# Group 0's rows of an MoE layer gathered on chip by one-hot products, with the other routes under its first expert

## The chip, the cores and the metric

The kernel runs on one core of a Trainium2 chip. The metric is device time in microseconds (us), the median of several executions. TensorE (PE) multiplies matrices, its weight loads are listed as PEld; VectorE is DVE, ScalarE ACT, GpSimd POOL, and SyncE (SP) issues most DMAs.

## What is computed

One layer of a decoder trunk on 512 tokens of 1024 features, all in fp32. A mixer (three branches and an output projection) gives a residual x1; then comes a mixture of experts in two steps. The most likely of 4 groups is chosen for a token, then 2 of its 4 experts:

```python
x = x + gt1 * mix
h2 = rms_norm(x, g_norm2) * (1.0 + sc2) + sh2
grp_prob = softmax(h2 @ w_group + b_group);  p_g, g_idx = top_k(grp_prob, 1)
sel_logits = (h2 @ w_router + b_router) of the 4 experts of g_idx
top_vals, e_idx = top_k(sel_logits, 2);  weights = p_g * softmax(top_vals)
for e in 16 experts:      # feature sizes 1024 -> 256 -> 1024
    y += (silu(h2 @ w_gate[e]) * (h2 @ w_up[e]) * combine[:, e]) @ w_down[e]
x = x + gt2 * y
```

`sc2`, `sh2`, `gt2` come from the condition c: a gain and a shift of each feature. With the inputs used, group 0 has 68 tokens, and no expert has more than two tiles of 128.

## The kernel before, in words

**Products.** fp32 products are exact enough in two ways. Either an operand is split into a high and a low fp32r half (`split`: ACT writes the high half, DVE subtracts to get the low one) and TensorE makes three passes (`mm3`, L216), or the operands stay fp32 ("native", one product listed as two records).

**The end of the mixer.** `out_mm(t, g, ...)` makes the block of token tile t (0 to 3) and output columns g (0 to 3) of the output projection; the order of blocks is the list `seq`, which ends (2, 2), (2, 3), (3, 2), (3, 3). After a block, `out_evac` (L1215, L1216) multiplies it by the gate and adds it to x1 on DVE; `x1_t` transposes a tile of x1 on TensorE (L1224) and ACT copies it (L1227); `logits` multiplies it by the router's weights, into which the gain is folded (L1236); `norm2` gives 1/rms of a token, rs2, whose power is taken on POOL (L1249); `norm_lg` scales the logits (L1252). `tile_chain(t)` is this series for one tile, put between blocks by a queue of generators (`wv`), a step or two behind the blocks. `h2_rows` makes half a tile of h2 rows (512 columns) and writes it to `h2_d` in DRAM; by its mode the work is on DVE, ACT or POOL (`h2_gain`, L1256, and L1275 are POOL's).

**The routes.** `route(t0)` finds group and experts of tiles t0 and t0 + 1 on DVE with some 15 small steps (L1290 to L1308). `ranks` (L1609, L1610) counts on TensorE, by products with a triangle and ones, which place a token has in its expert. Then DVE makes positions (L1654 to L1657), `weights` (L1312 to L1321) and `lightest` (L1640 to L1650: which of groups 1 to 3 has the fewest tokens; its experts share a tile at the end). `busy(n)` puts n products of ones between these steps on TensorE (L1399), whose result nobody reads; there are 41.

**The experts.** There are 17 passes e = 0 to 16. Passes 0 to 3 are the experts of group 0, pass 6 takes what overflows a tile, and passes 13 to 16 are the lightest group's, sharing a tile (`GL` = 13). For an expert with a tile of its own, `one_hot(e)` compares places with 0 to 127 on DVE (L1469); `slot_rows`/`slots` multiply it by token numbers and weights (L1477, L1488), and POOL gathers the rows from `h2_d` by an indirect DMA (L1481). `x_rows` transposes them, 8 transposes with a step of 8 elements (L1519), into `XTf` (native) or `XTh`/`XTl` (split). `gate_up` (L1535 or L216), `activate` (SiLU on ACT, L1543 on DVE), `act_t` (transpose of the activations, L1551), `down` (L1577 or L216), the scaling y (L1582) and an indirect DMA that adds the rows to the output (L1591) follow. `w_units` split the next expert's weights (L225, L226: `guh`, `gul`, `dnh`, `dnl`), pieces of 512 KB that SP loads in a fixed order into a ring of buffers (`load_raw`, L1167). Each engine takes its instructions strictly in the order in which the program's text emits them (`manual_schedule`), so the loop over e, which calls these parts in turn, is the order on every engine.

Of the kernel before, what the change touches and what calls it, by code (L numbers as in the profile page):

```python
# [35 lines left out]
PRE = 4  # L36
# [135 lines left out]
def trunk(ctx: ExitStack, tc: tile.TileContext, I, out, dbg=None):  # L172
# [793 lines left out]
    def mod_rows(hf):  # L966
# [18 lines left out]
        for j in range(4):  # L985
# [14 lines left out]
            if hf == (j < 2):  # L1000
                A.dma_start(mod_d[1 - hf:2 - hf, 512 * (j % 2):512 * (j % 2) + 512], bm[0:1])
            yield 1

    def router_consts():
        lst = sml("lst")[:, 0:128]
        A.dma_start(lst, I["cst"][:, C_LST:C_END])
        A.dma_start(R.mcol, mod_d.rearrange("a (k p) -> p a k", p=128))
        yield 5
# [8 lines left out]
        V.scalar_tensor_tensor(R.mcol[:, 0], R.mcol[:, 0], 1.0, pv[:, PV_G2:PV_G2 + 8], OP.add, OP.mult)  # L1017
# [165 lines left out]
    def f():  # L1183
# [17 lines left out]
        R.xg = pool("xgp", wps).tile([128, 1024], FT, name="xg")  # L1201
# [31 lines left out]
    def logits(t, ks, last=7, b=None):  # L1233
        b = b or bank()
        for k in ks:
            T.matmul(b[:, 0:27], xT.pop((t, k)), R.wrs[:, k], start=k in (0, 4), stop=k in (3, 7))  # L1236
        if 3 in ks:
            V.tensor_copy(R.LG[:, t], b[:, 0:27])
        elif 7 in ks:
            V.tensor_tensor(R.LG[:, t], R.LG[:, t], b[:, 0:27], OP.add)  # L1240
        return b
# [9 lines left out]
    def norm_lg(t):  # L1251
        V.scalar_tensor_tensor(R.LG[:, t], R.LG[:, t], R.rs2[:, t:t + 1], R.brb, OP.mult, OP.add)  # L1252

    def h2_gain(t, c0, n):
        c = slice(c0, c0 + n)
        G.tensor_tensor(R.xg[:, c], X1(t)[:, c], st["mod", 1][:, c], OP.mult)  # L1256

    def h2_rows(t, hf, mode):
        s = slice(hf * 512, hf * 512 + 512)
        s2 = slice(1024 + hf * 512, 1024 + hf * 512 + 512)  # L1260
        h2 = sml("h2")
        rs, sh = R.rs2[:, t:t + 1], st["mod", 0][:, s2]
        if mode[0] == "V":
            V.scalar_tensor_tensor(h2, X1(t)[:, s], rs, st["mod", 1][:, s], OP.mult, OP.mult)
        elif mode == "A":
            A.activation(h2, X1(t)[:, s], AF.Copy, scale=rs)
            G.tensor_tensor(h2, h2, st["mod", 1][:, s], OP.mult)
        elif mode == "gA":
            A.activation(h2, R.xg[:, s], AF.Copy, scale=rs)
        if mode == "gV":  # L1270
            V.scalar_tensor_tensor(h2, R.xg[:, s], rs, sh, OP.mult, OP.add)
        else:

            def end(eng=G):
                eng.tensor_tensor(h2, h2, sh, OP.add)  # L1275
                SY.dma_start(h2_d[t * 128:(t + 1) * 128, s], h2)
            if mode == "VV":
                return lambda: end(V)
            end()
            return  # L1280
        SY.dma_start(h2_d[t * 128:(t + 1) * 128, s], h2)
# [4 lines left out]
    def route(t0):  # L1286
# [3 lines left out]
        V.tensor_reduce(m1[:, :, 0:1], lg[:, :, 0:4], AX.X, OP.max)  # L1290
# [32 lines left out]
    def tile_chain(t):  # L1323
        x1_t(t, 512, 512)
        norm_pre(t)
        norm2(t)
        out_rows(t)
        yield 2 if t < 2 else 1
        logits(t, range(4, 8))
        norm_lg(t)  # L1330
        if t == 1:
            route(0)
        yield 1
        h2_rows(t, 1, "A" if t < 1 else "V")
        if t < 2:
            h2_rows(t, 0, "V")
        else:
            st["h2"] = h2_rows(t, 0, "VV")

    def last_half():  # L1340
        x1_t(3, 512, 256)
        h2_gain(3, 512, 256)
# [22 lines left out]
    def f():  # L1365
# [3 lines left out]
        for t, g in seq:  # L1369
# [27 lines left out]
    def busy(n):  # L1397
        for _ in range(n):
            T.matmul(wb, ones_c, ones_c[:, None, :].to_broadcast([128, 4, 128]), start=True, stop=True)  # L1399

    wb = bank("mm")
    lb = logits(3, (4, 5))
    busy(3)
# [59 lines left out]
    NE = 17  # L1463

    def one_hot(e, po=None):
        if po is None:
            po = R.PC[:, e, 0:4] if e < PRE else R.eb[:, 0:4] if e == EX else R.posx if e == EX + 1 else R.posL if e == GL else R.PP[:, wset(e) - PRE, 0:4]
# [5 lines left out]
    def slot_rows(e, b=None):  # L1473
# [21 lines left out]
    def slots(e):  # L1495
        if e < GL:
# [4 lines left out]
        for ti in range(NT):  # L1501
            T.matmul(b[:, 0:8], oh[:, ti], R.twL[:, ti], start=ti == 0, stop=ti == 3)
# [390 lines left out]
```

## Time and profile before

| | us |
|---|---|
| median of 3 runs | 809.42 (806.77 to 811.06) |
| the profiled execution | 806.46 |
| its span, first to last instruction | 804.6 |
| TensorE busy in the span | 759.2 (94%) |
| DVE busy | 558.0 (69%) |
| ACT busy | 313.5 (39%) |
| POOL busy | 177.8 (22%) |
| DMA, mean over the span | 185 GB/s |

The mean granted TensorE clock of the span is 0.985 of full speed. The page gives busy time per engine, a table of slices and groups of instructions; stretches and timelines are asked of the trace. Times in the rows count from the span's start. A record in brackets is the idle time before an instruction and what ended it.

### The profile page before, as it was taken

Reading aid. Unit: us, or ns where it says so; the run is one execution under the profiler, and the core shown is the slowest. Engines: PE = TensorE matmul, PEld = TensorE weight load, DVE = VectorE, ACT = ScalarE, POOL = GpSimd, SP = SyncE. Lnnn points to the kernel's source line nnn. Section 1 sums busy time; section 2 is a strip of 40 time slices with the busy share of each in tenths; the row PEclk is TensorE's granted clock in tenths of the full one; section 3 lists DMA queues with packets and bytes.
Section 4 is the critical chain, followed back from the end, with each engine's and each line's share of the span. In section 5 each row is a group of like instructions: output and inputs, shape, how many; then the busy total and the mean of one; then the engine's idle time right before and its main releaser. Section 6 shows DMA issues by size and latency. Waiting matters only on the chain. (4 is left out here: it accounts for less than half of the span.)

```text
span 804.6 us, 11741 instructions
## 1 busy us (share of the span) xinstructions
PE 759.2 (94%) x4261; PEld 628.2 (78%) x4262; DVE 558.0 (69%) x1046; ACT 313.5 (39%) x556; POOL 177.8 (22%) x162
## 2 busy tenths in 40 slices
PE   7699997999999999999899999999988999999994
PEld 4477986998888899998688887889975677777662
DVE  5987737778748776775777777745476788677761
ACT  5424743242334224322344333434212454355550
POOL 2522207422121013320110031300161223221100
PEclk9799999999999999999999999999989999999998
DMA  9882243221212121358445576597556999999931
GB/s 300 255 260 90 67 129 136 77 78 59 73 53 94 64 79 53 100 190 253 139 144 163 173 229 219 163 304 234 214 185 242 321 345 363 363 363 354 331 97 27
DMA packets 68596, 148.53 MB, mean 185 GB/s; under 512 B 8189, under 2 KB 35986, under 8 KB 68282
## 3 DMA queue, kind: packets, MB, share of 16 engines
q1 hardware_dynamic: 59234, 130.00, 47.4%
q0 software_dynamic: 4032, 14.68, 7.2%
q10 hardware_dynamic: 5272, 3.09, 1.4%
q8 instruction: 34, 0.56, 0.3%
q14 instruction: 24, 0.20, 0.1%
HBM read 136.21 MB, written 12.86 MB: 185 GB/s over the span
## 5 line engine op out<-in xcount | busy, mean ns | idle before, releaser
L226 DVE TENSOR_TENSOR wlo<-raw,whi 128x1024 fp32r<-128x1024 f32 x70 | 92.2, 1321 | 60.6 <-ACT whi L225 60.5
L216 PE MATMUL bank_mm<-whi,hTh 128*128 128x256 f32 x352 | 100.9, 287 | 0.0
L216 PE MATMUL bank_mm<-wlo,hTh 128*128 128x256 f32 x352 | 98.8, 281 | 1.8 <-DVE wlo L226 1.8
L216 PE MATMUL bank_mm<-whi,hTl 128*128 128x256 f32 x352 | 98.8, 281 | 0.0
L216 PE MATMUL bank_mm<-hTh,whi 128*128 128x512 f32 x224 | 92.4, 413 | 0.0
L225 ACT ACTIVATE whi<-raw 128x1024 fp32r<-128x1024 f32 x70 | 73.2, 1054 | 48.6 <-DMA raw<-in_w_t_dram 30.5
L216 PE MATMUL bank_mm<-hTh,wlo 128*128 128x512 f32 x224 | 88.9, 397 | 0.0
L216 PE MATMUL bank_mm<-hTl,whi 128*128 128x512 f32 x224 | 88.4, 395 | 0.0
L216 PEld LDWEIGHTS bank_mm<-wlo,hTh 128*128 128x128 f32 x352 | 66.4, 189 | 2.2 <-DVE wlo L226 2.0
L216 PEld LDWEIGHTS bank_mm<-whi,hTh 128*128 128x128 f32 x352 | 66.4, 189 | 0.6 <-issue 0.3
L216 PEld LDWEIGHTS bank_mm<-whi,hTl 128*128 128x128 f32 x352 | 66.3, 188 | 0.0
L216 PE MATMUL bank_mm<-whi,mgs 128*128 128x256 f32 x256 | 51.5, 295 | 0.2 <-DVE mgs L229 0.2
L216 PEld LDWEIGHTS bank_mm<-hTh,whi 128*128 128x128 f32 x224 | 42.2, 188 | 11.0 <-issue 1.0
L216 PEld LDWEIGHTS bank_mm<-hTh,wlo 128*128 128x128 f32 x224 | 42.1, 188 | 10.6 <-DVE wlo L226 0.5
L216 PEld LDWEIGHTS bank_mm<-hTl,whi 128*128 128x128 f32 x224 | 42.1, 188 | 10.0 <-issue 0.7
L216 PE MATMUL bank_ms<-dnh,aT 128*128 128x512 f32 x120 | 45.8, 441 | 0.0
L963 DVE SCALAR_TENSOR_TENSOR acc<-raw,c_act,acc 128x1024 f32<-128x1024 f32 x28 | 37.9, 1368 | 8.3 <-DMA raw<-in_w_mod_dram 7.9
L1591 POOL DMA_INDIRECT out_dram<-modb,idx x14 | 25.2, 1797 | 81.1 <-DVEq L1875 27.1
L216 PEld LDWEIGHTS bank_mm<-whi,mgs 128*128 128x128 f32 x256 | 42.6, 199 | 0.5 <-DVE mgs L229 0.4
L216 PE MATMUL bank_mm<-wlo,mgs 128*128 128x256 f32 x128 | 37.2, 291 | 0.0
L900 POOL TENSOR_TENSOR mg<-mg,ut 128x512 f32<-128x512 f32 x8 | 11.2, 1409 | 101.3 <-DVE ut L898 101.3
L1582 DVE SCALAR_TENSOR_TENSOR modb<-bank_ms,wsl,modb 128x512 f32<-128x512 f32 x26 | 19.5, 751 | 18.3 <-PE bank_ms L216 16.3
(439 smaller groups left out, 1798.0 us busy)
## 6 DMA issues: line engine op xcount, KB each, us to landing
raw<-in_w_t_dram SPq DMA_DIRECT2D x35, 512.0 KB, 3.5
raw<-in_w_mod_dram SPq DMA_DIRECT2D x32, 512.0 KB, 4.5
raw<-in_w_m_dram SPq DMA_DIRECT2D x24, 512.0 KB, 3.2
wmod<-in_w_mod_dram SPq DMA_DIRECT2D x16, 512.0 KB, 7.4
raw_x<-in_w_ed_dram SPq DMA_DIRECT2D x16, 512.0 KB, 9.2
raw_x<-in_w_eg_dram SPq DMA_DIRECT2D x15, 512.0 KB, 9.9
raw_x<-in_w_eu_dram SPq DMA_DIRECT2D x15, 512.0 KB, 8.5
raw_e<-in_w_eg_dram SPq DMA_DIRECT2D x14, 512.0 KB, 5.9
```

Of the source, the lines that this page charges most:

```text
L216: T.matmul(o, l[a], r[b], start=first and i == 0, stop=last and i == 2)
L225: A.activation(hi, src, AF.Copy)
L226: (eng or V).tensor_tensor(lo, src, hi.bitcast(FT), OP.subtract)
L900: G.tensor_tensor(m, m, u, OP.add)
L963: V.scalar_tensor_tensor(acc[:, c], raw, c_act[:, kt:kt + 1], acc[:, c], OP.mult, OP.add)
L1582: V.scalar_tensor_tensor(y[:, c], b, wsl_[e][:, 0:1], g, OP.mult, OP.mult)
L1591: G.indirect_dma_start(out, bass.IndirectOffsetOnAxis(idx_[e][:, 0:1], 0), y, None, compute_op=OP.add)
```

## The change

**Group 0 shares a tile.** Passes 0 to 3 work on one tile of group 0's tokens. `group(t)` marks on DVE which tokens of a tile have group 0, `group_ranks(t)` counts their places on TensorE, `group_hot(t)` makes on DVE a one-hot of token by place, already scaled by rs2. `gather(t)` multiplies x1 of the tile (stationary, columns k, k + 8, ...) by it, 8 products into two PSUM banks that add up over the four tiles; so the gathered rows come transposed, with no DMA and no transposes. `x_group` puts gain and shift on them with 8 ACT copies (`mcolx`, loaded by a DMA of its own), `x_halves` splits them for experts 1 to 3. The tile's 4 experts take its weights in `activate` (as the lightest group's do), their `down` products add up in the same two banks, and one scaling and one scatter follow after pass 3.

**The routes go under expert 0.** route(0) is called two blocks later, at (3, 2); route(2), the last ranks, positions, weights, lightest, the one-hot of pass 0 and the h2 rows of tiles 2 and 3 are emitted within pass 0, the steps of `overflow` in passes 0 and 1. Loads 16, 17, 20 and 21 are issued in the bridge, 18 and 19 after the h2 rows of tile 3.

**Row arithmetic.** `h2_rows` is on DVE alone, two steps for half a tile; `h2_gain` and `busy` are gone. POOL keeps the powers of rs2 and the indirect DMAs.

```diff
-    def h2_rows(t, hf, mode):
...
+    def h2_rows(t, hf):
         s = slice(hf * 512, hf * 512 + 512)
...
+        V.scalar_tensor_tensor(h2, X1(t)[:, s], R.rs2[:, t:t + 1], st["mod", 1][:, s], OP.mult, OP.mult)
+        V.tensor_tensor(h2, h2, st["mod", 0][:, 1024 + hf * 512:1536 + hf * 512], OP.add)
         SY.dma_start(h2_d[t * 128:(t + 1) * 128, s], h2)
+    def group(t):
+        m1 = R.MT[:, 0, t, 0:1]
+        V.tensor_reduce(m1, R.LG[:, t, 0:4], AX.X, OP.max)
+        V.tensor_tensor(R.gm[:, t], R.LG[:, t, 0:2], m1.to_broadcast([128, 2]), OP.is_equal)
+        V.tensor_scalar(R.pen[:, t:t + 1], R.gm[:, t, 0:1].bitcast(FT), -1024.0, 1024.0, OP.mult, OP.add)
+    def group_ranks(t):
...
+        for tj in range(t + 1):
+            T.matmul(st["rg"][:, 2 * t:2 * t + 2], R.lst if tj == t else ones_c, R.gm[:, tj], start=tj == 0, stop=tj == t)
+    def group_hot(t):
+        p0 = R.p0[:, t:t + 1]
+        V.tensor_tensor(p0, st["rg"][:, 2 * t:2 * t + 1], R.pen[:, t:t + 1], OP.add)
+        V.tensor_scalar(st["oh0"][:, t], R.cst[:, C_IOTA:C_IOTA + 128], p0, R.rs2[:, t:t + 1], OP.is_equal, OP.mult)
+    def gather(t, ks=range(8)):
...
+        for k in ks:
+            T.matmul(st["X0"][k // 4][:, (k % 4) * 128:(k % 4) * 128 + 128], X1(t)[:, k::8], st["oh0"][:, t],
+                     start=t == 0 and k % 4 == 0, stop=t == 3 and k % 4 == 3)
...
             if (t, g) == (3, 2):
                 wv.start(last_half(), 1)
+                route(0)
+                gather(0)
...
+    gather(1, range(5))
+    x1_t(3, 768, 256)
+    norm2(3)
+    gather(1, range(5, 8))
+    logits(3, (6, 7), b=lb)
+    norm_lg(3, lb)
+    group(3)
+    ranks((0, 1))
+    gather(2, range(3))
+    group_ranks(3)
+    group_hot(3)
+    gather(2, range(3, 8))
+    gather(3)
+    x_group()
+    out_rows(3)
+    for u in U:
+        u()
+    for j in (16, 17, 20, 21):
+        load_raw(j)
     route(2)
...
         gate_up(e, (0, 1))
         if e == 0:
+            x_halves()
         U[0]()
         U[1]()
+        if e == 0:
+            ranks((2, 3))
+            positions()
+            weights()
...
         gate_up(e, (2, 3))
         if e:
             act_t(e - 1)
+        if e == 0:
+            lightest()
...
+            one_hot(0)
...
         gate_up(e, (4, 5))
+        if e == 0:
+            slots(0)
+            h2_rows(2, 0)
+            h2_rows(2, 1)
...
         activate(e)
+        if e == 0:
+            h2_rows(3, 0)
+            h2_rows(3, 1)
+            for j in (18, 19):
+                load_raw(j)
...
+            one_hot(4)
```

Three places show what moved. First TensorE (PE) from the last ranks to the first gate_up products, before (L1477 are the index products, L1519 the transposes):

```order
L1399 MATMUL bank_mm<-ones_c 128x512 x8
L1477 MATMUL bank_ms<-tok,oh 128x4 x4
L1399 MATMUL bank_mm<-ones_c 128x512 x5
L1477 MATMUL bank_ms<-tok,oh 128x4 x4
L1399 MATMUL bank_mm<-ones_c 128x512 x12
L1519 MATMUL bank_ms<-ident,X 128x128 x8
L1477 MATMUL bank_ms<-tok,oh 128x4 x4
L1535 MATMUL bank_mm<-raw_e,XTf 128x512 x4
```

and from the last 13 gather products (L1282) through pass 0 with the change (L1613 and L1614 are `ranks((2, 3))`, L1547 `gate_up`, L1474 and L1499 `slots(0)`):

```order
L1282 MATMUL bank_ms<-oh_5545,x_5001 128x128 x13
L1547 MATMUL bank_mm<-raw_e,XTf 128x512 x2
L1613 MATMUL bank_mm<-mem,lst 128x20
L1613 MATMUL bank_mm<-mem,ones_c 128x20
L1614 MATMUL bank_mm<-mem,ones_c 128x20
L1613 MATMUL bank_mm<-mem,lst 128x20
L1614 MATMUL bank_mm<-mem,ones_c 128x20
L1547 MATMUL bank_mm<-raw_e,XTf 128x512 x2
L1547 MATMUL bank_mm<-raw_x,XTf 128x512 x2
L1474 MATMUL bank_ms<-tok,oh 128x4 x4
L1499 MATMUL bank_ms<-tw_4923,oh 128x8 x4
L1547 MATMUL bank_mm<-raw_x,XTf 128x512 x2
```

The gather stands directly ahead of the first gate_up; the last ranks and the slots stand behind gate_up products of pass 0, where TensorE waits for what DVE makes.

Second DVE at the residual add of block (2, 3), before (L1215, L1216): the whole of route(0), L1290 to L1308, stands between it and the add of block (2, 2).

```order
L1290 TENSOR_REDUCE MT<-LG 128x2
L1293 MATCH_REPLACE rt_g<-MT,LG 128x11 x2
L1295 TENSOR_TENSOR nmem<-rt_g,LG 128x2x4
L1297 SCALAR_TENSOR_TENSOR EL<-nmem,LG 128x16 x2
L1301 MAX rt_5577<-EL 128x8 x2
L1302 COPY MT<-rt_5577 128x2x2
L1305 MATCH_REPLACE rt_r<-MT,EL 128x22 x2
L1306 TENSOR_TENSOR mem<-rt_g,LG 128x2x4
L1307 TENSOR_TENSOR mem<-rt_r,EL 128x2x16
L1308 TENSOR_TENSOR nmem<-rt_r,EL 128x2x16
L1215 TENSOR_TENSOR mx_5599<-bank_mm,modb 128x256
L1216 TENSOR_TENSOR x_4999<-x_4999,mx_5599 128x256
```

and with the change, up to the same add (now L1214, L1215), where h2 rows of tile 0 (L1255, L1256), its one-hot (L1275, L1276) and tile 1's logits and group (L1249 to L1264) stand:

```order
L1256 TENSOR_TENSOR h_5547<-h_5547,modb 128x512
L1275 TENSOR_TENSOR p_4922<-bank_ms,pen 128x1
L1276 TENSOR_SCALAR oh_5545<-cst,p_4922,rs_4907 128x128
L1255 SCALAR_TENSOR_TENSOR h_5566<-x_5000,rs_4907,modb 128x512
L1256 TENSOR_TENSOR h_5566<-h_5566,modb 128x512
L1249 SCALAR_TENSOR_TENSOR LG<-LG,rs_4907,brb 128x27
L1250 SCALAR_TENSOR_TENSOR LG<-bank_ms,rs_4907,LG 128x27
L1262 TENSOR_REDUCE MT<-LG 128x1
L1263 TENSOR_TENSOR gm<-LG,MT 128x2
L1264 TENSOR_SCALAR pen<-gm 128x1
L1214 TENSOR_TENSOR mx_5592<-bank_mm,modb 128x256
L1215 TENSOR_TENSOR x_5001<-x_5001,mx_5592 128x256
```

route(0) comes after the add of block (3, 2), two blocks later.

Third DVE under expert 0 with the change, from the last h2 half row of tile 2 to the one-hot of pass 4 (L1466), for which `slots(4)` on TensorE waits. Before, these h2 rows stood at the end of the mixer, on DVE, ACT and POOL.

```order
L1256 TENSOR_TENSOR h_5907<-h_5907,modb 128x512
L1558 SCALAR_TENSOR_TENSOR act<-act,w_5900,bank_mm 128x256
L1255 SCALAR_TENSOR_TENSOR h_5916<-x_5001,rs_4907,modb 128x512
L1256 TENSOR_TENSOR h_5916<-h_5916,modb 128x512
L1255 SCALAR_TENSOR_TENSOR h_5920<-x_5001,rs_4907,modb 128x512
L1256 TENSOR_TENSOR h_5920<-h_5920,modb 128x512
L1649 CAST tw<-PP 128x8
L1650 TENSOR_TENSOR tw<-PP,tw 128x8
L1466 TENSOR_TENSOR oh<-cst,PP 128x512
```

The activation of pass 0 (L1558) stands between the h2 rows of tiles 2 and 3.

## Rows read from the trace of the kernel before

**Rows 1.** The page: busy time of each engine, its share of the span, its instructions.
```profile
PE 759.2 (94%) x4261; PEld 628.2 (78%) x4262; DVE 558.0 (69%) x1046; ACT 313.5 (39%) x556; POOL 177.8 (22%) x162
```

**Rows 2.** Stretches: length, busy of PE, PEld, DVE, ACT, POOL, granted clock, DMA share, GB/s.
```profile
25.90:30.00 4.10, 4.10 (x14) 2.81 (x15) 3.96 (x8) 2.71 (x3) 2.11 (x2) 0.61 0.82 241
585.80:588.90 3.10, 0.05 (x1) 0.05 (x1) 3.00 (x15) 0.01 (x1) 0.91 (x1) 1.00 0.45 169
590.00:596.00 6.00, 6.00 (x30) 6.00 (x30) 4.43 (x10) 0.54 (x3) 4.91 (x5) 0.50 0.60 199
624.00:784.00 160.00, 160.00 (x672) 113.10 (x672) 119.86 (x229) 82.53 (x142) 33.77 (x24) 1.00 0.94 318
```

**Rows 3.** Timeline of DVE, block (2,3): start, us, line, operation, out<-in, count.
```profile
585.55 1.28 DVE L1297 SCALAR_TENSOR_TENSOR EL<-nmem,LG 128x16 f32<-128x16 f32 x2
...
587.91 0.42 DVE L1215 TENSOR_TENSOR mx<-bank_mm,modb 128x256 f32<-128x256 f32 x1
588.37 0.43 DVE L1216 TENSOR_TENSOR x<-x,mx 128x256 f32<-128x256 f32 x1
```

**Rows 4.** Timeline, PE's waits over 3 us and POOL meanwhile; in brackets: idle, releaser.
```profile
25.85 0.61 PE L342 MATMUL bank_ms<-ones_c,macc 128*128 128x1 f32 x4 [3.30 <-DVE macc L337]
...
584.20 2.51 POOL L1275 TENSOR_TENSOR h<-h,modb 128x512 f32<-128x512 f32 x2
...
588.85 0.33 PE L1224 MATMUL bank_ms<-ident,x 128*128 128x128 f32 x1 [3.05 <-DVE x L1216]
```

**Rows 5.** Timeline of the bridge, ACT, POOL, DVE and PE.
```profile
599.28 0.38 ACT L1227 ACTIVATE x1T<-bank_ms 128x256 f32<-128x256 f32 x1
...
599.50 0.93 POOL L1249 TENSOR_TENSOR rs<-ms,mhalf 128x1 f32<-128x1 f32 x1 [2.92 <-DVE ms L1248]
...
603.30 0.26 DVE L1297 SCALAR_TENSOR_TENSOR EL<-nmem,LG 128x16 f32<-128x16 f32 x2
...
604.69 0.28 PE L1609 MATMUL bank_ms<-mem,lst 128*128 128x20 f32 x1 [0.96 <-DVE mem L1307]
...
613.37 1.16 PE L1519 MATMUL bank_ms<-ident,X 128*128 128x128 f32 x8 [0.91 <-DMA X<-h_d,idx]
...
614.76 1.55 PE L1535 MATMUL bank_mm<-raw_e,XTf 128*128 128x512 f32 x3
```

**Rows 6.** Timeline of PE, fp32 products of 128x128 in the mixer.
```profile
452.70 1.05 PE L1088 MATMUL bank_ms<-pT,dv 128*128 128x128 f32 x8
```

**Rows 7.** Weight loads 590 to 640 us by line: busy, mean ns, idle before.
```profile
L1535 PEld LDWEIGHTS bank_mm<-raw_x,XTf 128*128 128x128 f32 x16 | 2.8, 191 | 2.4 <-issue 2.4
...
L1519 PEld LDWEIGHTS bank_ms<-ident,X 128*128 128x128 f32 x16 | 2.0, 194 | 1.3 <-DMA X<-h_d,idx 1.3
```

**Rows 8.** Stretches of route results on DVE: positions, weights, lightest.
```profile
605.34:606.53 1.19, 1.19 (x7) 0.96 (x7) 1.02 (x4) 0.00 (x0) 0.00 (x0) 1.00 0.18 38
610.39:612.20 1.81, 1.81 (x9) 1.34 (x8) 1.43 (x9) 0.36 (x2) 0.96 (x1) 1.00 0.86 208
614.98:616.78 1.80, 1.80 (x5) 0.84 (x5) 1.62 (x11) 1.80 (x5) 0.94 (x1) 1.00 1.03 421
```

**Rows 9.** DVE by line, 590 to 640 us: busy, mean ns, idle before.
```profile
L226 DVE TENSOR_TENSOR gul<-raw_x,guh 128x512 fp32r<-128x512 f32 x8 | 5.1, 685 | 0.3 <-ACT guh L225 0.3
...
L1264 DVE SCALAR_TENSOR_TENSOR h<-x,rs,modb 128x512 f32<-128x512 f32 x3 | 2.2, 746 | 0.0
```

**Rows 10.** Timeline of PE: expert 1's transposes; first transpose of expert 2's activations.
```profile
619.97 1.13 PE L1519 MATMUL bank_ms<-ident,modb 128*128 128x128 f32 x8 [1.51 <-DMA modb<-h_d,idx]
...
650.67 0.27 PE L1551 MATMUL bank_ms<-ident,act 128*128 128x128 f32 x1
```

**Rows 11.** Tile raw_x, 740 to 790 us: durations, first and last start; landing times.
```profile
L225 ACT ACTIVATE guh<-raw_x x10: 618/621/1056, 744.1 to 783.4; 128x512 fp32r<-128x512 f32 x8, 128x1024 fp32r<-128x1024 f32 x2
...
L1167 SPq DMA_DIRECT2D raw_x<-in_w_ed_dram x4: 332/332/333, 752.8 to 761.3; - x4
...
DMA to landing us min/median/max: 9.1/10.4/10.5
```

More of the change, by code (lines that the diff above doesn't have):

```diff
@@ L1231, in x1_t, with logits @@
             xT[t, (c0 + i) // 128] = d[:, i:i + 128]
-    def logits(t, ks, last=7, b=None):
+    def logits(t, ks, b=None):
         b = b or bank()
@@ L1328, in tile_chain @@
         yield 2 if t < 2 else 1
[L1329 to L1332, printed above, removed]
+        norm_lg(t, logits(t, range(4, 8)))
+        group(t)
         yield 1
-        h2_rows(t, 1, "A" if t < 1 else "V")
+        group_ranks(t)
         if t < 2:
-            h2_rows(t, 0, "V")
-        else:
-            st["h2"] = h2_rows(t, 0, "VV")
+            h2_rows(t, 1)
+            yield 1
+        group_hot(t)
+        if t < 2:
+            h2_rows(t, 0)
     def last_half():
         x1_t(3, 512, 256)
-        h2_gain(3, 512, 256)
         yield 1
@@ L1463, in trunk, with one_hot @@
     NE = 17
-    def one_hot(e, po=None):
-        if po is None:
-            po = R.PC[:, e, 0:4] if e < PRE else R.eb[:, 0:4] if e == EX else R.posx if e == EX + 1 else R.posL if e == GL else R.PP[:, wset(e) - PRE, 0:4]
+    GR0 = range(4)
+    shared = lambda e: e in GR0 or e >= GL
+    first = lambda e: not shared(e) or e in (0, GL)
+    last = lambda e: not shared(e) or e in (GR0[-1], NE - 1)
+    def one_hot(e):
+        po = R.PC[:, 16, 0:4] if e == 0 else R.eb[:, 0:4] if e == EX else R.posx if e == EX + 1 else R.posL if e == GL else R.PP[:, wset(e) - PRE, 0:4]
         oh = sp_.tile([128, 512], FR, name="oh", tag="s").rearrange("p (t j) -> p t j", t=4)
@@ L1505, in slots, with x_group, x_halves @@
         V.tensor_tensor(w8[:, :, 0], w8[:, :, 0], w8[:, :, 1], OP.add)
-        wsl_[GL] = w8
+        wsl_[e] = w8
+    def x_group():
+        XT = [ep.tile([128, 4, 128], FT, name="XTf", bufs=2) for _ in range(2)]
+        for k in range(8):
+            A.activation(XT[k // 4][:, k % 4], st["X0"][k // 4][:, (k % 4) * 128:(k % 4) * 128 + 128], AF.Identity,
+                         bias=R.mcolx[:, 1, k:k + 1], scale=R.mcolx[:, 0, k:k + 1])
+        XT_[0] = [[x] for x in XT]
+    def x_halves():
+        XT = [ep.tile([128, 4, 128], FR, name="XT" + x, bufs=2) for x in "hl"]
+        split(XT[0], XT[1], XT_[0][0][0])
+        for e in GR0[1:]:
+            XT_[e] = [XT, XT_[0][1]]
     def x_rows(e):
+        if e in GR0:
+            return
         if e > GL:
@@ L1574, in down @@
             for k in range(2):
-                s0, s1 = e <= GL and k == 0, (e < GL or e == NE - 1) and k == 1
+                s0, s1 = first(e) and k == 0, last(e) and k == 1
                 if len(dn[k]) == 1:
@@ L1587, in down @@
                 load_raw(AT[wset(e), 4 + q] + NRAW)
-        if GL <= e < NE - 1:
-            return
-        e = min(e, GL)
-        G.indirect_dma_start(out, bass.IndirectOffsetOnAxis(idx_[e][:, 0:1], 0), y, None, compute_op=OP.add)
+        if last(e):
+            i = idx_[GL if e >= GL else 0 if e in GR0 else e]
+            G.indirect_dma_start(out, bass.IndirectOffsetOnAxis(i[:, 0:1], 0), y, None, compute_op=OP.add)
     U = w_units(0)
-    x1_t(3, 768, 256)
-    busy(3)
-    norm2(3)
-    st.pop("h2")()
-    h2_rows(3, 0, "gV")
-    out_rows(3)
-    h2_gain(3, 768, 256)
-    logits(3, (6, 7), b=lb)
-    norm_lg(3)
-    rb, cb = bank(), bank()
+    rb = bank("mm")
+    cb = rb[:, 80:100]
     def ranks(tm):
@@ L1800, in trunk @@
             U[7]()
-        if e < 1:
-            next(ov, None)
+        if e == 0:
+            for _ in range(3):
+                next(ov)
         DN = U[8:]
```

148 lines of the change are left out of this document (44 added, 104 removed).

## The prediction

> **What bounds the kernel now.** I read the page's engine line first [rows 1]: TensorE is busy 759.2 of 804.6 us, so only its 45 idle us, its work and its clock can be gained. Then the table by stretches [rows 2], where the change begins and after it: in 585.8 to 588.9 us TensorE works 0.05 of 3.10 us; in 590 to 596 it is busy throughout, at a granted clock of 0.50 (1.2 instead of 2.4 GHz); from 624 to 784, under the experts, it is busy 160.00 of 160.00 us at 1.00. So a gain must come from before 624, and a lead that TensorE has after the first experts it carries to the end, if weights come in time. Last I read the timelines at those places for what ended each wait.
>
> Two places matter. **Place A**, the end of the out-projection: VectorE runs route(0) and only then, at 587.91, the residual add of a finished block [rows 3]; TensorE's transposes of that block wait 3.05 us for it [rows 4], and the half clock of [rows 2] follows. GpSimd's row arithmetic (2.51 us, [rows 4]) runs beside route(0): the step L1297 takes 1.28 us for two there [rows 3] and 0.26 in route(2) [rows 5]. **Place B**, the bridge to expert 0: the last rs2 begins at 599.50, ranks wait for route(2) until 604.69, the eight transposes wait for rows by indirect DMA until 613.37, and the first gate_up starts at 614.76 [rows 5].
>
> A difference under 0.5% (4 us) is about what a measurement of this kernel can't tell from none. The sum is made against the profiled execution, 806.46 us, of which 804.6 are its span. The median of the runs shown is 809.42, 3.0 us above it; I take the gain off that median.
>
> **Place A, costed.** Up to about 577 us the order of work is the same. route(0) now stands two blocks later and no row arithmetic on GpSimd beside it, so the residual add is in time: the 3.05 us wait goes, and so does the half clock behind it, under which 590 to 597 held some 3.5 us of full-clock work less. New on TensorE are group ranks and the 8 products of gather(0). A 128x128 fp32 product takes 0.22 us (8 records, two to a product, in 1.05 us less the last one's run-out, [rows 6]), so gather(0) is 1.76 us; some ten small products add 0.7, an estimate from two records' 0.22 there. New waits: group_ranks(1) and group_ranks(2) stand in TensorE's own queue behind a block's products and need logits, rs2 (0.93 on GpSimd, [rows 5]) and four VectorE steps; I put 1.3 and 1.1 us on them. Behind them queue out_mm blocks; nobody else waits. Sum: 3.05 + 3.5 - 1.76 - 0.7 - 1.3 - 1.1 = 1.7; I take **1.5 us**, with bounds 0 (waits of 2 us each) and 4 (no waits).
>
> **Place B, costed.** Off TensorE's path go the 41 fillers (they only filled waits), the wait for route(2), index products, the landing of the rows and 8 transposes. Added are 24 products, 5.3 us, of which gather(1) and half of gather(2) lie in waits for x1, logits and group(3), and 8 copies on ACT, some 0.2 us each (half of the 0.38 for twice the size, [rows 5]). The chain: rs2 ends at 600.43 [rows 5], 1.5 us earlier is 598.9; scaled logits, group and group_ranks(3) some 2.0, to 600.9; group_hot(3) 0.5, beside it the last five products of gather(2), 1.1, to 602.0; gather(3) 1.76, to 603.75, with the first four copies beside its second half. So the first gate_up comes at about 603.75 instead of 614.76 [rows 5], **11.0 us** earlier. Bounds: 8 (all in series) and 12.5.
>
> **Under expert 0**, where the moved work goes, VectorE sets the pace. From XTl at 605.35: XTl 0.68 like a gul piece, gul twice 1.3 [rows 9], positions 1.2, weights 1.8, lightest 1.8 [rows 8], a one-hot 0.69 (same size), and small steps between. What slots(0) needs is ready at 612.75 (its one-hot) and 613.1; TensorE arrives at 609.45 and waits **3.3 us**. gate_up(1) starts at 615.4, which is 10.75 us earlier than before. Next on VectorE stand h2 of tiles 2 and 3, four half rows of 0.75 for the product [rows 9] and some 0.68 for the add, between them the activation (behind SiLU on ACT), and the one-hot of expert 4, ready at 621.65. TensorE arrives at slots(4) at 618.45 and waits **3.2 us** again. Behind it queue the rest of gate_up(1) and GpSimd's gather for expert 4, which is not used until two experts later. Experts 1 and 2 need no transposes: 0.9 us each (8 records in 1.16 with the last one's run-out, [rows 5]), and the old wait of 1.51 for expert 1's rows [rows 10] lies before the start of gate_up(1) and is counted in the 10.75. So 10.75 - 3.2 + 1.8 = 9.35, less 0.25 for the products of the group's weights: act_t of expert 2 comes at 641.6 instead of 650.67 [rows 10], a lead of **9.1 us**. From expert 3 on the order is the same.
>
> **The clock.** The waits of 3.30 and 3.05 us [rows 4] were followed by a clock of 0.61 and 0.50 [rows 2]. So the first new wait may halve the clock for some 7 us too, a loss of about 3.5 us. But the wait behind it is VectorE's: a slower TensorE comes later to slots(4) and waits less there, and nearly all of the loss disappears in the 3.2 us; that leaves 8.9. **The likeliest: 809.42 - 8.9 = 800.5 us.** Edits at no cost: the h2 half rows on VectorE at place A lie beside busy TensorE (out_mm covers them; without it 1.4 us each); three scatters and four gathers less, as GpSimd and the queues are idle there for most of the time; the DMA of mcolx goes out beside mcol's, long before.
>
> The stationary operand of every gather product steps by 8 elements. The weight loads with the same step, L1519's, take 194 ns, packed ones (L1535) 191 [rows 7], so I price the products as packed. The Trainium skill speaks against them: "SBUF — State Buffer", Specifications (TRN2), says that reads need two hits per 16-byte line for full bandwidth, which a step of 8 fp32 never has. By that rule the time would be rival 3's; these loads show next to nothing of it.
>
> **The rivals.**
> 1. *The clock falls behind the second wait alone, or stays low for longer* (0.20). If the first wait is under 3 us and the second isn't, nothing absorbs the loss: 9.1 - 3.5 = 5.6, **803.8 us**. For: both waits above 3 us in [rows 4] had it. Against: the first wait is as long. The Trainium skill's "TensorE: Matmul & The Clock Gate" (Part 1) says that the moment of switching varies from run to run; by that, runs of one kernel could fall to either case.
> 2. *The weight stream becomes the bound* (0.10). Loads 18 and 19 go out on SP only after the last h2 half row, at about 621, and all later ones behind them. Before, the last loads go out up to 761.3, land 9.1 to 10.5 us later and are used up to 783.4 [rows 11], a slack of about 11 us, with the DMA engines busy 0.94 of 624 to 784 [rows 2]. A lead of 9 leaves 2, and the transfers saved return some. If the stream is 6 us late all the same, the lead is 5: **804.5 us**.
> 3. *The gather is dearer or later than costed* (0.08). Each product twice as long is 24 x 0.22 = 5.3 us on the bridge and 1.76 at place A: the lead falls to about 2, **807.5 us**, no change that can be told. For: no row shows an fp32 product with a stepped operand. Against: [rows 7].
> 4. *VectorE under expert 0 is stretched* (0.07, the other side). From XTl to the one-hot of expert 4 it has 16.3 us. Beside GpSimd's arithmetic a step took five times as long [rows 3, 5]. If that stage took 1.8 times as long, 13 us more, TensorE would wait for it, and the lead of 8.9 would turn into 4.1 us lost: **813.5 us**. It decides from a one-hot later than 630.5 on. Against: GpSimd has no arithmetic left there.
>
> **How the numbers follow.** The forecast has 0.55, its own range 797 to 803: the bounds at A and B reach the end damped, since VectorE's chain, not the first gate_up, sets TensorE from slots(0) on. Faster by more than 0.5% (below 805.4): 0.55, 0.18 of rival 1, 0.07 of rival 2, together 0.80. Within 0.5%: 0.02 + 0.03 + 0.08 = 0.13. Slower: 0.07. The range, 796.5 to 806, leaves out rivals 3 and 4 and a little of the others.
>
> **What would show it.** Right: no 3 us wait and a clock of 1.00 in 585 to 597; the first gate_up at 603 to 605; two waits of TensorE for VectorE's one-hots under experts 0 and 1, of 3 us each, or one with a low clock behind it and little of the other; act_t of expert 2 some 9 us earlier, and then the same distances between experts with no wait for DMA. Wrong: waits above 2 us at group_ranks; a first gate_up after 607; the one-hot of expert 4 after 625; waits for weights under late experts; a clock below 1.00 beyond 630.

## The result, and the profile after

The changed kernel takes 816.76 us (median of 7 runs, 815.08 to 818.64) where the kernel before took 807.18 us beside it (7 runs, 803.40 to 811.06). The ratio is 1.011, with a 95% interval of 1.0078 to 1.0142: slower by about 9 us, where 8.9 us faster was forecast. The profiled execution of the change took 818.61 us, its span is 816.9 us. Its line of engines on the page, beside [rows 1]:

```profile
PE 765.0 (94%) x4243; PEld 635.1 (78%) x4243; DVE 554.0 (68%) x1053; ACT 311.7 (38%) x555; POOL 156.8 (19%) x145
```

TensorE has 18 records less and is busy 5.8 us longer. To see where, I took from the timelines the starts of the same steps: the first and the last block product of the output projection, the first gate_up, and the first transposes of the activations of experts 0, 1, 2 and 4 (act_t). The distances between them, in us, for both kernels and for the experiments below:

| | output projection | bridge | expert 0 | to act_t of 1 | of 2 | of 4 |
|---|---|---|---|---|---|---|
| before | 63.2 | 17.3 | 14.2 | 11.2 | 10.5 | 21.1 |
| the change | 69.8 | 14.5 | 17.9 | 11.2 | 9.9 | 23.1 |
| k1, mcolx alone | 67.2 | 17.9 | 13.7 | 11.2 | 10.5 | 21.1 |
| k2, swap | 63.2 | 14.5 | 17.8 | 11.8 | 9.8 | 23.1 |
| k3, swap, fillers in the bridge | 62.0 | 16.3 | 16.3 | 12.3 | 9.8 | 23.1 |
| k4, swap, ranks moved | 62.2 | 13.1 | 17.9 | 11.7 | 9.8 | 23.1 |
| k5, swap, packed gather | 60.8 | 8.1 | 18.1 | 12.0 | 9.8 | 23.1 |
| k6, packed gather, weights to match | 61.6 | 8.1 | 18.2 | 11.9 | 9.8 | 23.0 |
| k7, k6 with fillers in the waits | 60.6 | 8.1 | 15.2 | 13.4 | 9.9 | 23.1 |
| k8, k6 with another bank | 60.6 | 8.1 | 18.4 | 11.3 | 9.8 | 21.1 |
| k9, k8 with late slots | 60.0 | 8.1 | 16.5 | 10.5 | 10.3 | 21.1 |
| k10, k7 with another bank | 60.1 | 8.1 | 15.1 | 13.4 | 9.9 | 21.1 |
| k11, k9 with fillers | 60.3 | 8.1 | 14.8 | 11.6 | 10.8 | 21.1 |

From act_t of expert 4 to the start of TensorE's last product every kernel takes the same, 121.3 us. The change's profiled execution also begins the output projection 3.8 us later than that of the kernel before, where next to nothing is changed; k5, the same program up to there, begins it 1.4 us earlier than the kernel before, so this is a difference between executions. In the first column too, executions of the same order of work differ by up to 1.7 us (k6 to k11).

Four places answer to the rows of before. **First, a wait that I had not seen coming.** The timeline of the change at the start of the output projection (ACTq is ScalarE's queue, issuing DMAs):

```profile
541.13 0.39 ACTq L1007 DMA_DIRECT2D mcol<-mod_d  x1
...
541.57 7.46 ACTq L1008 DMA_DIRECT2D mcolx<-mod_d  x1
...
549.08 0.63 ACT L228 ACTIVATE mgs<-ut 128x512 fp32r<-128x512 f32 x1 [9.19 <-DMA x<-in_x_dram]
...
549.76 0.58 PE L216 MATMUL bank_mm<-whi,mgs 128*128 128x256 f32 x1 [6.19 <-ACT mgs L228]
```

The issue of the new DMA alone holds ScalarE for 7.46 us. Behind it stands the last split of the mixer's sum (mgs), and TensorE waits 6.19 us for that. The bracket of L228 names a DMA of x, because a semaphore of it came last; the row above it shows what held the engine.

**Second, the gather.** The timeline of TensorE in the bridge, and the weight loads there by line (mean ns behind the bar):

```profile
607.89 0.28 PE L216 MATMUL bank_mm<-whi,mgs 128*128 128x256 f32 x1
...
608.37 2.62 PE L1282 MATMUL bank_ms<-oh,x 128*128 128x128 f32 x10
...
616.13 6.43 PE L1282 MATMUL bank_ms<-oh,x 128*128 128x128 f32 x26
...
622.40 1.88 PE L1547 MATMUL bank_mm<-raw_e,XTf 128*128 128x512 f32 x4
```

```profile
L1282 PEld LDWEIGHTS bank_ms<-oh,x 128*128 128x128 f32 x64 | 15.7, 334 | 0.0
...
L1223 PEld LDWEIGHTS bank_ms<-ident,x 128*128 128x128 f32 x32 | 4.0, 155 | 0.0
```

26 records, two to a product, take 6.43 us: 0.49 us a product, where [rows 6] gave 0.22. One weight load of the gather takes 334 ns. TensorE has no wait in the bridge at all; it is the bound there.

**Third, the waits under the experts**, TensorE's rows with a wait behind the first gate_up:

```profile
631.58 0.58 PE L1474 MATMUL bank_ms<-tok,oh 128*128 128x4 f32 x4 [3.31 <-DVE tw L1649]
...
641.37 0.58 PE L1485 MATMUL bank_ms<-tw,oh 128*128 128x4 f32 x4 [0.65 <-DVE k L1700]
...
663.37 0.58 PE L1485 MATMUL bank_ms<-twx,oh 128*128 128x4 f32 x4 [0.72 <-DVE aT L226]
...
674.89 0.61 PE L1485 MATMUL bank_ms<-twx,oh 128*128 128x4 f32 x4 [0.73 <-DVE aT L226]
```

The first was forecast at 3.3 us. The second was forecast at 3.2, or next to nothing if the clock fell behind the first. The last two were not forecast.

**Fourth, the clock.** Stretches with the columns of [rows 2]:

```profile
549.80:554.00 4.20, 4.20 (x20) 3.98 (x21) 3.91 (x6) 1.88 (x3) 0.00 (x0) 0.55 0.20 54
616.00:620.00 4.00, 4.00 (x18) 4.00 (x18) 2.31 (x19) 0.00 (x0) 0.00 (x0) 0.50 0.96 330
632.00:636.00 4.00, 4.00 (x11) 2.35 (x10) 3.88 (x9) 0.00 (x0) 0.00 (x0) 0.51 0.57 156
597.00:612.00 15.00, 15.00 (x100) 15.00 (x99) 8.96 (x40) 2.90 (x9) 1.10 (x2) 1.00 0.27 106
```

It is half behind both long waits, and whole at the end of the output projection (597 to 612). It is also half at 616, behind no wait. It fell at 615.0:

```profile
612.84 0.26 PE L1613 MATMUL bank_mm<-mem,lst 128*128 128x20 f32 x1
...
613.85 1.77 PE L1282 MATMUL bank_ms<-oh,x 128*128 128x128 f32 x6
...
614.00:615.00 1.00, 1.00 (x5) 1.00 (x6) 0.00 (x0) 0.00 (x0) 0.00 (x0) 0.99 0.87 233
615.00:616.00 1.00, 1.00 (x7) 1.00 (x6) 0.00 (x0) 0.00 (x0) 0.00 (x0) 0.50 0.95 266
```

Up to then TensorE had done the ranks (20 columns) and first products of gather(2) without a gap.

### The profile page after: what moved, and what is told of

Same layout as the page of the kernel before. It is cut to its first block, busy times and chain, and to the rows that moved or that the text cites. A ratio compares the mean times of both kernels' runs of the same rounds, so it can differ in the third digit from the quotient of the medians.

```text
span 816.9 us, 11668 instructions
## 1 busy us (share of the span) xinstructions
PE 765.0 (94%) x4243; PEld 635.1 (78%) x4243; DVE 554.0 (68%) x1053; ACT 311.7 (38%) x555; POOL 156.8 (19%) x145
## 5 line engine op out<-in xcount | busy, mean ns | idle before, releaser
L216 PEld LDWEIGHTS bank_mm<-hTh,wlo 128*128 128x128 f32 x224 | 42.1, 188 | 10.3
L1603 POOL DMA_INDIRECT out_dram<-modb,idx x11 | 20.9, 1904 | 71.0 <-DVEq L1883 25.6
L216 PE MATMUL bank_mm<-guh,XTh 128*128 128x512 f32 x64 | 32.6, 509 | 0.0
L1547 PE MATMUL bank_mm<-raw_x,XTf 128*128 128x512 f32 x64 | 32.1, 629 | 0.0
```

What stands on the lines that cost most here:

```text
L216: T.matmul(o, l[a], r[b], start=first and i == 0, stop=last and i == 2)
L1547: T.matmul(gb[e], x[0][:, kt % 4], w[0][:, kt % 2], start=kt == 0, stop=kt == 7)
L1603: G.indirect_dma_start(out, bass.IndirectOffsetOnAxis(i[:, 0:1], 0), y, None, compute_op=OP.add)
```

## The experiments

Ratios are to the kernel before, run on the same chip at the same time.

**k1, the DMA alone.** To the kernel before, one line (and its tile):

```diff
         A.dma_start(R.mcol, mod_d.rearrange("a (k p) -> p a k", p=128))
+        A.dma_start(R.mcolx, mod_d.rearrange("a (p k) -> p a k", k=8))
```

> The kernel before with one line more: the DMA of mcolx, issued by ScalarE right behind that of mcol (nothing reads it). Theory A (ScalarE's queue: mcolx's issue must wait until mcol's 2048 four-byte pieces have drained, ScalarE stands meanwhile and TensorE waits for the last mgs): the issue takes some 7.5 us, TensorE waits some 6 us at the start of the output projection and has half clock for some 7 us behind it, in all about 9.5 us slower than before (ratio 1.012). Rival A2 (the wait comes from another part of the change, the DMA is free): no change, ratio 1.000 to 1.002.

Measured: 1.0097 (1.0066 to 1.0128), 7.8 us. Its timeline:

```profile
536.58 7.28 ACTq L1008 DMA_DIRECT2D mcolx<-mod_d  x1
...
544.58 0.58 PE L216 MATMUL bank_mm<-whi,mgs 128*128 128x256 f32 x1 [6.30 <-ACT mgs L228]
```

Theory A holds in the place and the size of the wait: one DMA that nothing reads costs 7.8 us. That mcolx waits for mcol's pieces to drain is not shown by it. The cost came out below 9.5. Part of the difference lies at the end of the output projection: this execution also waits 3.08 us for the residual add behind route(0), as [rows 4] does, but the clock behind it stays whole, where [rows 2] shows 0.50:

```profile
594.67 0.44 PE L1225 MATMUL bank_ms<-ident,x 128*128 128x128 f32 x2 [3.08 <-DVE x L1217]
...
594.70:600.20 5.50, 5.50 (x47) 5.49 (x48) 5.00 (x10) 1.99 (x6) 3.69 (x4) 1.00 0.32 123
```

**k2, the two DMAs swapped** in the changed kernel:

```diff
-        A.dma_start(R.mcol, mod_d.rearrange("a (k p) -> p a k", p=128))
         A.dma_start(R.mcolx, mod_d.rearrange("a (p k) -> p a k", k=8))
+        A.dma_start(R.mcol, mod_d.rearrange("a (k p) -> p a k", p=128))
```

> The changed kernel with the two DMAs swapped: mcolx first, mcol behind it. Theory A: mcolx's issue takes under 0.5 us, no wait of TensorE for mgs and no half clock in the 20 us after it; 9.5 us faster than the change, so about the time of before (ratio to before 0.997 to 1.003). Rival A3 (mcolx's own pattern is slow to issue, wherever it stands): ScalarE stands as long, ratio to before 1.010 as with the change.

Measured: 1.0038 (1.0020 to 1.0056). Against the change's 1.011 that is 0.72%, 5.8 us (some 2.8 to 8.8 by the two intervals). In the first column of the table it is 6.6 us (7.8 and 7.6 in k3 and k4, which have the swap too). The issue of mcolx is now short, and TensorE's wait for ScalarE's mgs is gone:

```profile
L1007 ACTq DMA_DIRECT2D mcolx<-mod_d x1: 402/402/402, 538.9 to 538.9; - x1
```

So it is not the pattern of mcolx but its place behind mcol, whose pieces are four bytes each. Rival A3 falls. What holds the issue inside the queue no run here shows. The kernel is still 3 us slower than before, so more than this was wrong.

**k3, fillers in the bridge.** On the swap:

```diff
...
     ranks((0, 1))
+    busy(4)
     gather(2, range(3))
     group_ranks(3)
+    busy(2)
```

`busy` is defined again, on a bank of its own (left out here).

> As the swap, with six of the removed filler products back in the bridge: four behind ranks of tiles 0 and 1, two behind the group ranks of tile 3. Theory B (the granted clock fell to 0.50 during the gather because TensorE did only short products of 2 to 27 columns just before, where before there were fillers): 1.3 us of fillers, but the 0.50 during the last gather products goes, 3.4 us, so some 2 us faster than the swap. Rival B2 (the fall has another cause, such as the 1.2 us wait for the group marks): 0.50 stays, 1.3 us slower than the swap.

Measured: 1.0057 (1.0035 to 1.0078). The bridge is 1.8 us longer. The clock fell all the same, as the fillers began, and came back sooner:

```profile
601.80:605.20 3.40, 3.40 (x14) 3.02 (x13) 0.00 (x0) 0.00 (x0) 0.00 (x0) 0.53 0.97 233
```

The last 26 gather records come after that stretch and take 6.24 us at full clock. So what theory B wanted to win back was not there to be won; the times of k2 and k3 can't be told apart.

**k4, ranks moved under expert 0.** On the swap:

```diff
-    ranks((0, 1))
...
-            ranks((2, 3))
+            ranks((0, 1, 2, 3))
```

> As the swap, with the ranks of tiles 0 and 1 moved from the bridge under expert 0, beside those of tiles 2 and 3. Theory C (TensorE itself is the bound in the bridge, every product ahead of the group ranks of tile 3 delays the first gate_up): the first gate_up comes 1.0 us earlier, counted from the end of the output projection; with theory B also true, the clock stays at 1.00 and it comes some 4 us earlier. Rival C2 (the bridge waits for VectorE's and ScalarE's chain, as the prediction had it): no change of the first gate_up.

Measured: 1.0014 (0.9992 to 1.0036). The bridge is 1.4 us shorter, so TensorE's own work is its bound (theory C). The clock stays at 1.00, and that decides between price and clock: the same 26 records, here at full clock, and in k2 with the clock down.

```profile
602.44 6.43 PE L1282 MATMUL bank_ms<-oh,x 128*128 128x128 f32 x26
...
602.40:608.60 6.20, 6.20 (x28) 6.20 (x28) 2.31 (x19) 1.50 (x4) 0.00 (x0) 1.00 0.92 295
```

```profile
606.55 6.43 PE L1282 MATMUL bank_ms<-oh,x 128*128 128x128 f32 x26
...
606.50:612.80 6.30, 6.30 (x27) 6.30 (x28) 2.32 (x19) 1.51 (x4) 0.00 (x0) 0.60 0.69 246
```

6.43 us both times. So the pace of the gather does not follow the array's clock. That its weight loads set it is what k5 tries.

**k5, packed reads.** On the swap:

```diff
-            T.matmul(st["X0"][k // 4][:, (k % 4) * 128:(k % 4) * 128 + 128], X1(t)[:, k::8], st["oh0"][:, t],
+            T.matmul(st["X0"][k // 4][:, (k % 4) * 128:(k % 4) * 128 + 128], X1(t)[:, 128 * k:128 * k + 128], st["oh0"][:, t],
```

> The swap, with the gather's stationary operand read packed (columns 128k to 128k + 127 instead of k, k + 8, ...). The features then stand in another order than group 0's weights, so group 0's part of the output is not the reference's; the work is the same. Theory D (the weight loads with a step of 8 take 334 ns where packed ones take 191, so a gather product takes 0.49 us instead of 0.22): 24 x 0.27 = 6.4 us off the bridge and 2.1 off the output projection, in all 8 us faster than the swap (ratio to before 0.994). Rival D2 (the products are slow because of fp32, or the low clock): less than 2 us.

Measured: 0.9946 (0.9919 to 0.9973), 7.4 us faster than the swap (some 4.8 to 10.0 by the two intervals). The weight loads take 192 ns, the 26 records 3.15 us, the bridge 8.1 us:

```profile
L1282 PEld LDWEIGHTS bank_ms<-oh,x 128*128 128x128 f32 x64 | 7.6, 192 | 0.0
```

```profile
598.77 3.15 PE L1282 MATMUL bank_ms<-oh,x 128*128 128x128 f32 x26
```

Theory D holds with its number. The clock does not fall in this bridge, without any filler.

**k6, packed, with weights to match.** On the changed kernel, k5's edit, no mcolx, and the weights of experts 0 to 3 loaded in the same order of features:

```diff
-        A.dma_start(R.mcolx, mod_d.rearrange("a (p k) -> p a k", k=8))
...
+        if j < 96 and SEQ[j][0] < PRE and i < 4:
+            src = I[("w_eg", "w_eu")[i % 2]][e].rearrange("(k p) f -> p k f", p=128)[:, 4 * hf:4 * hf + 4]
+            eng.dma_start(raws[j].rearrange("p (k f) -> p k f", k=4), src)
+            return
...
-                         bias=R.mcolx[:, 1, k:k + 1], scale=R.mcolx[:, 0, k:k + 1])
+                         bias=R.mcol[:, 1, k:k + 1], scale=R.mcol[:, 0, k:k + 1])
```

> The same with the reference's result: the gate and up weights of experts 0 to 3 are loaded with feature 128k + p on partition p (runs of 1 KB in DRAM instead of 4 KB), gain and shift come from mcol, and the DMA of mcolx is gone. Theories A and D: as the packed one, ratio to before 0.994, and ScalarE's queue free at the start of the output projection. Rival E (loads in shorter runs are slower and come late): waits of TensorE or ScalarE for group 0's weights, 1.000 or more.

Measured: 0.9949 (0.9926 to 0.9972). The stages are those of k5, and there is no wait for a weight: rival E falls.

**k7, fillers in the two waits.** On k6:

```diff
...
+        if e == 1:
+            busy(13, rb)
         if e + 3 <= GL and e:
             slots(e + 3)
...
         if e == 0:
+            busy(13, wb)
             slots(0)
```

`busy` (its definition is left out here) now takes the bank that it writes to.

> As the one before, with 13 filler products ahead of each of the two places where TensorE waits for a one-hot under experts 0 and 1. Theory F (the half clock behind the first wait is absorbed by the second, as the prediction had it): the clock stays at 1.00 under experts 0 and 1, and the time falls by no more than 1 us. Rival F2 (the half clock is paid in full): some 3.5 us faster.

Measured: 0.9914 (0.9888 to 0.9941). The clock is whole:

```profile
606.00:630.00 24.00, 23.14 (x91) 15.26 (x89) 21.53 (x70) 8.85 (x16) 1.90 (x1) 1.00 0.65 214
```

From the first gate_up to act_t of expert 1 it takes 28.6 us, in k6 30.1. So of the half clock behind the first wait 1.5 us reached act_t of expert 1: more than the 0.2 of the prediction and the 1 us of theory F, less than half of F2's 3.5. The comparison of the times (0.35%, the intervals overlap) does not say it alone.

The trace of k6 shows where they come from. VectorE's own chain to the one-hot of expert 4 waits for products that TensorE makes at half clock, 0.44 us for the weights of slots(0) and 0.90 us for the activation of expert 0 (behind ScalarE's SiLU, L1556, which waits for gate_up); first k6, then k7, where neither wait is left:

```profile
614.75 0.17 DVE L1504 COPY w<-bank_ms 128x8 f32<-128x8 f32 x1 [0.44 <-PE bank_ms L1502]
...
618.37 0.38 ACT L1556 ACTIVATE act<-bank_mm 128x256 f32<-128x256 f32 x1 [6.62 <-PE bank_mm L1550]
...
618.79 0.48 DVE L1561 SCALAR_TENSOR_TENSOR act<-act,w,bank_mm 128x256 f32<-128x256 f32 x1 [0.90 <-ACT act L1556]
```

```profile
615.30 0.47 DVE L1561 SCALAR_TENSOR_TENSOR act<-act,w,bank_mm 128x256 f32<-128x256 f32 x1
```

The one-hot begins 19.1 us after the first gate_up in k6 and 17.6 in k7.

**k8, another bank.** On k6, in `slot_w`:

```diff
-        b, oh = bank(), oh_.pop(e)
+        b, oh = bank("mm"), oh_.pop(e)
```

> As the right one, with the slots' products of experts 4 to 12 in a bank of the other pool of PSUM. Theory G (the two added waits of 0.7 us under experts 3 and 4, L1485 for aT, come from PSUM: two of five banks are held by group 0's sums, so the slots' products get the bank that aT has just been read from): both waits go, and the two distances of 11.5 us between experts become 10.5, 2 us faster. Rival G2 (VectorE is late there): no change.

Measured: 0.9899 (0.9859 to 0.9939). The waits for aT are gone, and the distances of act_t of experts 2, 3 and 4 are those of before; first the change, then k8:

```profile
661.36 0.39 PE L1564 MATMUL bank_ms<-ident,act 128*128 128x128 f32 x2
...
672.88 0.39 PE L1564 MATMUL bank_ms<-ident,act 128*128 128x128 f32 x2
...
684.43 0.39 PE L1564 MATMUL bank_ms<-ident,act 128*128 128x128 f32 x2
```

```profile
642.44 0.39 PE L1567 MATMUL bank_ms<-ident,act 128*128 128x128 f32 x2
...
652.98 0.39 PE L1567 MATMUL bank_ms<-ident,act 128*128 128x128 f32 x2
...
663.51 0.39 PE L1567 MATMUL bank_ms<-ident,act 128*128 128x128 f32 x2
```

11.5 and 11.5 became 10.5 and 10.5. Theory G holds: 2.0 us came from PSUM. The interval of the time overlaps with k6's.

**k9, late slots.** On k8:

```diff
-        if e + 3 <= GL and e:
+        if e + 3 <= GL and e > 1:
             slots(e + 3)
...
-            slots(0)
             h2_rows(2, 0)
...
         gate_up(e, (6, 7))
+        if e == 0:
+            slots(0)
+        if e == 1:
+            slots(4)
         activate(e)
```

> The right one with the slots' bank of the other pool, and slots(0) put behind the last gate_up products of pass 0, slots(4) behind those of pass 1. Theory H (the two waits under experts 0 and 1 are a matter of where the slots stand in TensorE's queue: VectorE has their one-hots only 3 to 4 us after TensorE arrives, and nothing behind them in the queue needs them): the first wait falls to 2 us or less, the second goes, no half clock follows, some 4 to 5 us faster than with the bank alone, ratio to before 0.984 to 0.986. Rival H2 (VectorE's chain sets the start of gate_up of expert 1 and the activations anyway): the waits move to the transposes of the activations, under 1.5 us faster.

Measured: 0.9885 (0.9861 to 0.9910), median 795.67 us beside 804.45. Of the two waits one is left, of 2.12 us, with half clock behind it:

```profile
610.31 0.76 PE L1477 MATMUL bank_ms<-tok,oh 128*128 128x4 f32 x4 [2.12 <-DVE tw L1652]
...
610.50:616.50 6.00, 6.00 (x19) 5.03 (x19) 5.76 (x12) 0.12 (x1) 0.00 (x0) 0.50 0.67 206
```

From the first gate_up to act_t of expert 2 it takes 2.4 us less than k8 (37.2 for 39.6); by the ratios it is 0.14%, within the intervals. Neither H's 4 to 5 us nor a pure H2.

**k10, k7 and k8 together.** Both edits as above.

> The right one with the fillers ahead of both waits and the slots' bank of the other pool. If theories F and G are both right they add up: 1.5 and 2.0 us off the right one, ratio to before 0.990 or a little less. If the waits for a bank only hid another wait, less.

Measured: 0.9887 (0.9864 to 0.9911). The stages add up: expert 0 as in k7, experts 2 to 4 as in k8.

**k11, fillers in the wait that k9 leaves.** On k9:

```diff
         if e == 0:
+            busy(9, wb)
             slots(0)
```

> The one with late slots, and nine filler products (2.0 us) ahead of slots(0), in the wait of 2.1 us that is left. Theory I (that wait alone halved the clock for 7 us behind it, and nothing absorbs it now): clock at 1.00 under expert 0, the first transposes of activations some 2.5 to 3 us earlier, ratio to before 0.984 to 0.986. Rival I2 (VectorE's chain up to the activation sets them anyway): a wait for act takes the place, under 1 us.

Measured: 0.9888 (0.9865 to 0.9911), as k9. The clock stays whole there and act_t of expert 0 comes 1.7 us earlier, but in the place of the half clock TensorE waits for the activations of experts 0 and 1, and by act_t of expert 2 nothing of that is left:

```profile
618.21 0.50 PE L1567 MATMUL bank_ms<-ident,act 128*128 128x128 f32 x2 [1.23 <-DVE act L1561]
...
629.76 0.47 PE L1567 MATMUL bank_ms<-ident,act 128*128 128x128 f32 x2 [0.97 <-DVE act L1561]
```

That is rival I2: VectorE's chain, with the h2 rows in it, sets this stage. k9, k10 and k11 can't be told apart; each beats both kernels.

## Why the prediction was wrong, by its steps

**The step that failed first: "the DMA of mcolx goes out beside mcol's, long before", at no cost.** I counted the DMA's landing, which nothing waits for, and not its issue, which stands in ScalarE's own order. Behind it stands work that TensorE needs. The change less the swap is 0.72%, 5.8 us; alone on the kernel before it is 7.8 us (5.3 to 10.3). "Up to about 577 us the order of work is the same" left out ScalarE's queue, in which the new DMA stands at 541.6.

**The second: "so I price the products as packed".** The price of 0.22 us a product was wrong by a factor of 2.2, and swap and packed gather differ by 0.9%, 7.4 us. Rival 3 named the mechanism, with 7.1 us, and I gave it 0.08. The mistake is in how [rows 7] were read. L1519 are transposes; their loads of 194 ns must be held against those of packed transposes, not against packed loads of products. The kernel before has those too, 400 to 640 us:

```profile
L1224 PEld LDWEIGHTS bank_ms<-ident,x 128*128 128x128 f32 x32 | 3.9, 155 | 4.4 <-DVE x L1216 4.4
```

Read so, the row showed that the step costs a load something. How much it costs an fp32 product no row of before showed (k5 gives it: 334 ns to 192), and the upper bound should have carried more weight. The rule of the Trainium skill that I weighed against the row ("SBUF — State Buffer", Specifications (TRN2): full bandwidth needs two hits per 16-byte line) spoke for the slower read, and here it agrees with the measurement.

**Place A was right but for that price.** The 3.05 us wait and the half clock behind it are gone (rows above, 597 to 612). Of the two waits for group marks, put at 1.3 and 1.1 us, one is left, of 1.22:

```profile
596.42 0.27 PE L1271 MATMUL bank_ms<-gm,lst 128*128 128x2 f32 x1 [1.22 <-DVE gm L1263]
```

With the DMA out of the way the output projection takes 62.0 to 63.2 us (k2 to k4), with packed reads as well 60.0 to 61.6 (k5 to k11). Forecast were 61.7, 1.5 less than before.

**The bridge came out as long as forecast with packed reads, but not for the reason given.** It takes 8.1 us in k5 to k11; the prediction's own numbers give 7.75 (from 597.5 less 1.5 to 603.75). The prediction had it wait for VectorE's chain from rs2 to group_hot(3), with gather(1) and half of gather(2) inside the waits. There are no such waits: in k5, VectorE has the group marks of tile 3 ready at 597.5, and TensorE comes to the product that needs them at 598.66, busy without a gap before.

```profile
597.32 0.16 DVE L1263 TENSOR_TENSOR gm<-LG,MT 128x2 fp32r<-128x2 f32 x1
...
598.66 0.25 PE L1271 MATMUL bank_ms<-gm,lst 128*128 128x2 f32 x1
```

TensorE's own work is the bound in both forms, and that the lengths agree to 0.4 us is in part luck. My first guess at its length after the result, the clock, was wrong: k3 and k4 show that the stepped gather takes as long at either clock.

**"From expert 3 on the order is the same"** was true of the order, not of the banks: `down` of experts 0 to 3 adds up in two of five PSUM banks, and the slots' products then get a bank that VectorE is still reading. 2.0 us (k8).

**The clock.** The first wait under expert 0 was 3.3 us as forecast, and the clock fell as forecast. The second wait shrank to 0.65 us, which was the mechanism of absorption. But its size was off: 1.5 us remained instead of 0.2 (k7). The step that failed is "the wait behind it is VectorE's": I took VectorE's chain as independent of TensorE's clock, and it waits for TensorE's products itself, 0.44 and 0.90 us in k6. In the change, where only the second of these two waits occurs (0.90), the one-hot of expert 4 was ready 18.8 us after the first gate_up instead of 17.9.

**What adds up.** From 8.9 us faster to 9.6 slower are 18.5 us. The DMA's issue 5.8, the stepped reads 7.4, the bank 2.0 and the half clock 1.5 make 16.7. The rest of 1.8 is within the intervals. The stages of the change's own profile, held against the forecast ones, give as much: the output projection is 8.1 us longer than forecast (69.8 for 61.7), the bridge 6.8 (14.5 for 7.75), the way from the first gate_up to act_t of expert 2 1.1 (39.0 for 37.85) and experts 3 and 4 2.0, together 18.0. A further cause could be that I counted as saved 3.5 us of half clock at the end of the output projection, which k1 does not have behind the same wait; that was not tried by itself. Nor is it needed in the account by stages, which is that of one execution. The Trainium skill's "TensorE: Matmul & The Clock Gate" (Part 1) says that the moment of switching varies from run to run; the kernel before agrees in that its mean granted clock was 0.973 to 0.990 in the 32 runs beside k1 to k4. Whether it has its half clock in all of them is open, since only one of its runs left a trace.

**The other rivals.** The weight stream did not become the bound: no wait of TensorE for a weight above 0.4 us under the experts in any kernel, up to the lead that k9 has. VectorE was not stretched under expert 0: TensorE had what slots(0) waits for 9.2 us after the first gate_up, forecast were 9.0 to 9.4.

## What to carry to other kernels

Cost a DMA twice: its landing for who reads it, and its issue for the engine that issues it and for all that stands behind it there, here behind a DMA in four-byte pieces on the same queue. Price an operation from a row of the same kind and the same access; where only one of the two agrees, keep both ends in the sum, and not just in a rival. When sums are held in PSUM over several steps, count which banks the steps between still have. Before one engine's wait is said to absorb another's delay, look whether its chain waits for that other engine itself.

## What the runs showed of the hardware

- The issue of a DMA of 256 pieces took 7.3 to 7.5 us on ScalarE directly behind one in 2048 four-byte pieces, and 0.40 to 0.61 us ahead of it (k2 to k5).
- Weight loads of fp32 products of 128 columns took 334 ns when the operand steps by 8 elements and 192 when packed. The 26 records took 6.43 us with the step, at a clock of 1.00 and of 0.60, and 3.15 packed (at 1.00). Loads of transposes with the same step had 194 against 155 ns, with no effect on their pace (8 stepped ones in 1.16 us, [rows 5]; 4 packed ones, L1082, in 0.60).
- The clock fell behind a wait of 2.12 us (k9) and did not behind one of 3.08 (k1), in one trace each. It also fell while TensorE was never idle, in runs with ranks among stepped gather products (the change, k2, k3); without those ranks (k4) or with packed reads (k5 to k11) it stayed at 1.00 in the bridge. What makes it fall there is open.
- Products of 128x4 waited 0.72 and 0.73 us for a PSUM bank from which VectorE had still to read, with two of five banks held by sums; in a bank of the other pool they did not (k8).
